# A two-block transformer kernel on one core: thirty-odd elementwise passes of the second block change from GpSimd to VectorE

## The chip, the cores and the metric

The kernel runs on 1 core of one Trainium2 chip. The metric is the device time of one execution in microseconds (us). The core has TensorE (PE in the profile, its weight loads PEld), VectorE (DVE), ScalarE (ACT), GpSimd (POOL) and SyncE (SP, which only issues DMAs here); ACT issues some DMAs too.

## The reference, cut to what matters

The reference is two blocks on 256 tokens of width 1024, all in float32. The first block has two layers, each a mixer and a product-key expert layer (PEER) with layer norms between them. The second block, whose mixer this change is about, is one layer:

```python
h = rmsnorm(x, g_mix[i])
u = h @ w_in[i]                      # rwkv columns, mla columns, gates
y_rw = rwkv7_time_mix(u_rw, ...)     # a recurrence over 256 steps, both directions
y_mla = mla_mix(u_mla, ...)          # 8 heads of attention
merged = gates[:, :, 0] * (y_rw @ w_br_rwkv[i]) + gates[:, :, 1] * (y_mla @ w_br_mla[i])
x = x + merged @ w_out[i]
x = x + peer_ffn(rmsnorm(x, g_ffn[i]), ...)
x = x + (p[i] @ w_ple_proj[i]) * jax.nn.sigmoid(rmsnorm(x, g_ple[i]) @ w_ple_gate[i])
```

In `rwkv7_time_mix` the projection `u` is first mixed with its two neighbours in time, `u + mu * (0.5 * (prev + next) - u)`, and the recurrence per head and direction is

```python
state = state * w_t + sa * b_t + v_t * k_t      # sa = state @ a_t
out_t = state @ r_t
```

with `a = -kk`, `b = kk * a`, decays `w`, and `kk` a normalized `k`.

## The kernel before, in words

**Split weights.** Every large product runs as three float32r matmuls: a weight tile `raw` is split into a high half `whi` (a cast on ACT, L111) and a low half `wlo = raw - whi` (a subtraction, L113), and TensorE adds whi·xhi, whi·xlo and wlo·xhi. `split(raw, lo)` at L106 takes a letter: "v" puts the subtraction on VectorE, anything else on GpSimd. `tm_halves` and `tm` (L183 and L191) pass a string of such letters that is gone through in turn. `raw` has 2 buffers of 2048 columns, `whi` and `wlo` 4 buffers each of 1024 columns.

**The end of the first block.** `layernorm` (L290) with `then` set goes over the two token halves tb = 0, 1: residual and statistics on VectorE (L299 to L302), four passes of scale and shift (L312, L313), then an rms norm whose transposed halves become `x` (`rmsnorm_tb`, `transposed_tb`). After tb = 0 it calls `ple_proj` (L277), which multiplies the per-layer embedding by two weight splits, and splits the four weight pieces of the mla projection ahead of their use (L318).

**The second block's projections.** `block2` loads eight pieces of `rw_fm` and splits each into two (the last into one): `weights(i)` at L660 names the engine. `shifted(i, dst)` at L666 runs the matmuls of piece i into a bank of PSUM, splits piece i + 1 ahead, copies the bank to `up` on ACT (L674) and does the neighbour mix on VectorE (L675 to L680). `cut` calls it for k, r and v, and between these calls the start of the first `prep` and the normalization `unit` are issued.

**The recurrence.** It is done in four rounds (two directions by two token halves). `prep(d, tb)` at L802 makes a round's operands: decays (`lw`, a scan `b`, exponentials `e3`), `AR` (L841 and L842), `bt` (L845, L846), `kt` (L856 to L858) and a running `ksum` (L860). `batch` at L885 inverts a triangular system per half of the heads by four doublings, each a mask on GpSimd (L922, L925), matmuls on TensorE (L928, L933), an addition on VectorE (L934) and a transpose (L938). `rwkv` at L1041 interleaves the two `batch` generators of a round with the `prep` of the next round; every third step it also advances the attention (`mla`, L1083).

**The order.** Each engine runs its own instructions strictly in the order in which they stand in its queue; the framework sets that order from the dependencies as it records the program, so that moving an operation to another engine also shifts its neighbours. A wait at the head of a queue holds all behind it.

Of the kernel before, what the change touches and what calls it, by code (L numbers as in the profile page):

```python
# [42 lines left out]
class Kern:  # L43
# [233 lines left out]
    def ple_proj(self, half, W):  # L277

        self.pd = self.dram.tile([4, 128, 512], F32, name="pd", tag="pd")
        pT = [t.rearrange("p (c t) -> p c t", c=2) for t in self.p_halves]  # L280
        for d in range(2):
            p = [self.bank("a") for _ in range(2)]
            self.tm(p, W["ple_proj"][d:d + 1], pT, "p")
            for tb in range(2):
                t = half("proj")
                self.nc.scalar.copy(t, p[tb])
                self.nc.sync.dma_start(self.pd[tb * 2 + d], t)

    def layernorm(self, half, h, acc, W, layer, k, then=None):

        nc = self.nc
# [3 lines left out]
        for tb in range(2):  # L295
            z = h[tb]
            st = self.strm.tile([128, 2, 6], F32, name="lnst", tag="lnst", bufs=2)
            for d in range(2):
                nc.vector.scalar_tensor_tensor(z[d], z[d], ALPHA, acc[tb][d], op0=ALU.mult, op1=ALU.add)  # L299
                nc.vector.bn_stats(st[:, d], z[d])  # L300
            mv = self.strm.tile([128, 3], F32, name="lnmv", tag="lnmv", bufs=2)
            nc.vector.bn_aggr(mv[:, 0:2], st.rearrange("p a b -> p (a b)"))  # L302
            self.rstd(mv[:, 1:2], 1e-5)
            if then is None:
                nc.vector.scalar_tensor_tensor(mv[:, 2:3], mv[:, 0:1], -1.0, mv[:, 1:2], op0=ALU.mult, op1=ALU.mult)
                self.scaled(z, z, mv[:, 1:2], mv[:, 2:3])
                n = 2 * layer + k
                self.transposed_tb(half, z, x, tb, self.lnc[:, n, 0], self.lnc[:, n, 1])
                self.store_h(tb, h, (layer, k))
            else:  # L310
                for d in range(2):
                    nc.vector.scalar_tensor_tensor(z[d], z[d], mv[:, 0:1], grow[d], op0=ALU.subtract, op1=ALU.mult)  # L312
                    nc.vector.scalar_tensor_tensor(z[d], z[d], mv[:, 1:2], brow[d], op0=ALU.mult, op1=ALU.add)  # L313
                self.rmsnorm_tb(half, h, x, tb, then)
                self.store_h(tb, h)
                if tb == 0:
                    self.ple_proj(half, W)
                    self.mla_halves = list(self.tm_halves(W["mla_tm"], "p", 416))  # L318
        return x

    def rms_scale(self, half, h, tb):
# [295 lines left out]
    def block2(self, x, W):  # L617
        nc = self.nc
        sub, add, mul = ALU.subtract, ALU.add, ALU.mult
        mm = nc.tensor.matmul  # L620
        with ExitStack() as st:
# [37 lines left out]

            def weights(i):  # L660
                raw = self.load(W["rw_fm"][i]) if i < 7 else self.load(W["rw_last"], 1024)
                return [self.split(raw[:, k * 1024:k * 1024 + 1024], "pv"[k] if i else "vp"[k]) for k in range(2 if i < 7 else 1)]

            ahead = [weights(0)]

# [136 lines left out]
            def prep(d, tb):  # L802
# [36 lines left out]
                yield  # L839
                AR = mx.tile([128, 4, 2, 128], F32, name="AR", tag="AR", bufs=2)  # L840
                nc.vector.scalar_tensor_tensor(AR[:, :, 0], lw, -1.0, kkT[tb], op0=mul, op1=mul)  # L841
                nc.gpsimd.tensor_tensor(AR[:, :, 1], b, rT[tb], op=mul)  # L842
                yield
                bt, kt = g4("bt"), g4("kt")
                nc.gpsimd.tensor_tensor(flat(bt), flat(kkT[tb]), flat(a), op=mul)  # L845
                nc.gpsimd.tensor_tensor(flat(bt), flat(bt), flat(e3), op=mul)  # L846
                yield
                for f in range(4):
                    nc.vector.tensor_scalar(a[:, f], a[:, f], 1.0, k_a[:, f:f + 1], op0=sub, op1=mul)
# [7 lines left out]
                yield  # L857
                nc.vector.tensor_tensor(flat(kt), flat(kd), flat(e3), op=mul)  # L858
                if not fresh:
                    nc.gpsimd.tensor_tensor(flat(ksum[tb]), flat(ksum[tb]), flat(kd), op=add)  # L860
                yield
                AY = [gran("AY").rearrange("p (f a c) -> p f a c", f=2, a=4) for _ in range(2)]
                Bt, Kt = [gran("Bt") for _ in range(2)], [gran("Kt") for _ in range(2)]
# [836 lines left out]
```

## Time and profile before

| what | value |
| --- | --- |
| median of 3 runs | 3317.68 us (3301.85, 3317.68, 3320.57) |
| the profiled execution, its own time | 3306.54 us |
| its span, first to last instruction | 3304.8 us |
| mean granted clock of TensorE | 0.977 of full speed |
| busy: PE, PEld, DVE, ACT, POOL | 95%, 86%, 76%, 49%, 28% of the span |

The profile names a group by line, engine, operation and tiles (out<-in), with its count, busy time, mean, and the idle time of the engine just before it with what ended that idle time ("<-"). A timeline row is: start in us from the span's start, duration in us, engine, line, operation, tiles, shape, count of instructions merged into the row, and in brackets an idle time before it. The duration of a row runs from when the engine took the instruction to its end, so that time in which an engine sits on an instruction that cannot proceed is in it.

The second block's mixer lies between 1960 us and about 2345 us of the span. Everything before it is the first block, and what follows is the gates, the output projection, the second block's PEER layer and the tail.

### The profile page before, as it was taken

How to read it: one execution, taken by the hardware profiler on the slowest of the kernel's cores; microseconds unless marked ns; L12 is line 12 of the kernel's file. 1: busy time of each engine (PE TensorE's matmuls, PEld its weight loads, DVE VectorE, ACT ScalarE, POOL GpSimd, SP SyncE). 2: the span in 40 equal slices, each digit the busy share in tenths (PEclk: the TensorE clock that was granted, in tenths of full speed). 3: DMA queues.
4: the chain of work that ended last, by engine and by line, in shares of the span. 5: the costliest groups of instructions: out<-in, count | busy, mean ns of one | idle time of the engine just before them, and what ended most of it. 6: DMA issues, size and time to landing. Idle time of an engine off the chain costs nothing.

```text
span 3304.8 us, 56194 instructions
## 1 busy us (share of the span) xinstructions
PE 3151.0 (95%) x22652; PEld 2827.8 (86%) x22652; DVE 2510.2 (76%) x4203; ACT 1631.2 (49%) x2450; POOL 916.4 (28%) x424
## 2 busy tenths in 40 slices
PE   8999999999999999999999997889999999999998
PEld 7899888887888799988887877778789998888887
DVE  6687989897456696888898556654569698999855
ACT  5554444444455554544444445554455444444445
POOL 1610132234213540023324223242143003323230
PEclk9999999999999999999999998999999999999999
DMA  5455555555653456565556653000455555655664
GB/s 214 166 202 203 193 195 205 198 203 201 226 199 129 153 181 214 189 208 193 195 195 220 220 181 141 1 1 14 166 179 184 211 193 195 207 199 199 231 210 156
DMA packets 119525, 592.24 MB, mean 179 GB/s; under 512 B 14304, under 2 KB 14688, under 8 KB 59104
## 3 DMA queue, kind: packets, MB, share of 16 engines
q1 hardware_dynamic: 96768, 549.18, 48.1%
q10 hardware_dynamic: 22496, 39.47, 3.2%
q8 instruction: 177, 2.90, 0.3%
q14 instruction: 84, 0.69, 0.1%
HBM read 548.23 MB, written 40.37 MB: 178 GB/s over the span
## 4 chain that ended last, share of the span: by engine, by line
PE 68%; DVE 17%; DMA 6%; POOL 3%; ACT 3%; issue 3%; ACTq 0%; DVEq 0%; SPq 0%; POOLq 0%
PE ps_b L119 10%; PE ps_a L1537 10%; PE ps_b L121 10%; PE ps_b L120 10%; PE ps_a L1539 10%; PE ps_a L1538 9%; DVE wlo L113 3%; DVE A L1435 2%; DMA raw<-u 2%; DVE clo L1466 2%; PE ps_c L1448 2%; POOL wlo L113 2%; DMA back<-away 1%; DVE Z L1443 1%; ACT whi L111 1%
## 5 line engine op out<-in xcount | busy, mean ns | idle before, releaser
L111 ACT CAST whi<-raw 128x1024 fp32r<-128x1024 f32 x941 | 976.6, 1048 | 1244.3 <-DMA raw<-v 318.2
L113 POOL TENSOR_TENSOR wlo<-raw,whi 128x1024 fp32r<-128x1024 f32 (+1 forms) x294 | 767.0, 2623 | 1945.6 <-ACT whi L111 1358.4
L121 PE MATMUL ps_b<-xThi,wlo 128*128 128x256 f32 x3608 | 1029.9, 285 | 29.1 <-POOL wlo L113 16.1
L119 PE MATMUL ps_b<-xThi,whi 128*128 128x256 f32 x3608 | 1034.6, 287 | 10.4 <-ACT whi L111 8.8
L120 PE MATMUL ps_b<-xTlo,whi 128*128 128x256 f32 x3608 | 1027.8, 285 | 0.3 <-DVE xTlo L144 0.3
L113 DVE TENSOR_TENSOR wlo<-raw,whi 128x1024 fp32r<-128x1024 f32 x647 | 804.2, 1247 | 223.3 <-ACT whi L111 219.9
L121 PEld LDWEIGHTS ps_b<-xThi,wlo 128*128 128x128 f32 x3608 | 699.0, 194 | 31.9 <-POOL wlo L113 17.7
L119 PEld LDWEIGHTS ps_b<-xThi,whi 128*128 128x128 f32 x3608 | 699.5, 194 | 15.5 <-ACT whi L111 9.0
L120 PEld LDWEIGHTS ps_b<-xTlo,whi 128*128 128x128 f32 x3608 | 699.0, 194 | 4.6 <-DVE xTlo L144 0.6
L1537 PE MATMUL ps_a<-whi,chi 128*128 128x512 f32 x1536 | 620.0, 404 | 0.3 <-ACT chi L1464 0.3
L1539 PE MATMUL ps_a<-whi,clo 128*128 128x512 f32 x1536 | 609.8, 397 | 6.0 <-DVE clo L1466 6.0
L1538 PE MATMUL ps_a<-wlo,chi 128*128 128x512 f32 x1536 | 608.4, 396 | 0.2 <-DVE wlo L113 0.2
L1539 PEld LDWEIGHTS ps_a<-whi,clo 128*128 128x128 f32 x1536 | 290.3, 189 | 75.5 <-DVE clo L1466 7.3
L1435 DVE TENSOR_TENSOR A<-iota,comb 128x2048 f16<-128x2048 f16 x192 | 330.1, 1719 | 21.4 <-PE ps_c L1448 21.2
L1538 PEld LDWEIGHTS ps_a<-wlo,chi 128*128 128x128 f32 x1536 | 290.9, 189 | 62.6 <-DVE wlo L113 0.5
L1537 PEld LDWEIGHTS ps_a<-whi,chi 128*128 128x128 f32 x1536 | 291.1, 190 | 61.7 <-ACT chi L1464 0.5
L1466 DVE TENSOR_TENSOR clo<-back,chi 128x512 fp32r<-128x512 f32 x126 | 159.5, 1266 | 88.4 <-ACT chi L1464 86.0
L1443 DVE TENSOR_TENSOR Z<-B,comb 128x512 f16<-128x512 f16 x384 | 204.7, 570 | 0.0
L1462 DVE TENSOR_TENSOR back<-back,G 128x512 f32<-128x512 f32 x126 | 100.2, 798 | 89.2 <-DMA back<-away 89.2
L1453 DVE SCALAR_TENSOR_TENSOR G<-ps_c,G 128x256 f32<-128x256 f32 x384 | 150.0, 414 | 21.2 <-ACT G L1452 20.2
L1537 PE MATMUL ps_a<-whi,xThi 128*128 128x512 f32 (+1 forms) x320 | 132.0, 413 | 14.6 <-ACT xThi L180 14.1
L1452 ACT ACTIVATE G<-ps_c 128x256 f32<-128x256 f32 x384 | 134.0, 378 | 11.2 <-PE ps_a L1539 0.4
(517 smaller groups left out, 3359.1 us busy)
## 6 DMA issues: line engine op xcount, KB each, us to landing
raw<-u SPq DMA_DIRECT2D x192, 1024.0 KB, 4.9
raw<-v SPq DMA_DIRECT2D x192, 1024.0 KB, 4.8
away<-gone ACTq DMA_DIRECT2D x126, 256.0 KB, 2.3
back<-away SPq DMA_DIRECT2D x126, 256.0 KB, 2.7
raw<-wq SPq DMA_DIRECT2D x24, 1024.0 KB, 4.8
raw<-c_tm SPq DMA_DIRECT2D x8, 1024.0 KB, 4.8
raw<-c_fm SPq DMA_DIRECT2D x8, 1024.0 KB, 4.8
raw<-gates_tm SPq DMA_DIRECT2D x8, 1024.0 KB, 4.8
```

The source lines that it names most:

```text
L111: self.nc.scalar.copy(hi, raw)
L113: eng.tensor_tensor(low, raw, hi.bitcast(F32), op=ALU.subtract)
L119: mm(out, whi, xhi, start=start, stop=False, skip_group_check=True)
L120: mm(out, whi, xlo, start=False, stop=False, skip_group_check=True)
L121: mm(out, wlo, xhi, start=False, stop=stop, skip_group_check=True)
L1435: nc.vector.tensor_tensor(A, self.iota2.unsqueeze(1).to_broadcast([128, 16, 64, 2]), cv[:, 0].to_broadcast([128, 16, 64, 2]), op=eq)
L1443: nc.vector.tensor_tensor(Z[:, :, i], B, cv[:, 2 + i].to_broadcast([128, 16, 16, 2]), op=mul)
L1453: nc.vector.scalar_tensor_tensor(Gt, pv[:, 1], 2.0 ** -15, Gt, op0=mul, op1=add)
L1466: nc.vector.tensor_tensor(clo, C, chi.bitcast(F32), op=sub)
L1537: mm(out, xhi, whi, start=start, stop=False, skip_group_check=True)
L1538: mm(out, xhi, wlo, start=False, stop=False, skip_group_check=True)
L1539: mm(out, xlo, whi, start=False, stop=stop, skip_group_check=True)
```

## The change

Four edits, in the second block's mixer and the end of the first block's last layer norm:

- `ple_proj` (L283) and the mla pieces (L318) split with "v" in place of "p": two subtractions of 128x1024 and four of 128x832 change from GpSimd to VectorE.
- `weights` (L662) calls `split` without a letter, which means VectorE: eight subtractions of 128x1024 change over, seven stay on VectorE as before.
- In `prep`, the products of L842, L845 and L846 change over, in each of four rounds.
- The addition to `ksum` (L860) changes over, in the two rounds that have it.

GpSimd keeps the masks (L922, L925), the memsets, the state's addition (L1024) and the products of `finish` (L1062, L1065).

```diff
@@ ple_proj
-            self.tm(p, W["ple_proj"][d:d + 1], pT, "p")
+            self.tm(p, W["ple_proj"][d:d + 1], pT)
@@ layernorm
-                    self.mla_halves = list(self.tm_halves(W["mla_tm"], "p", 416))
+                    self.mla_halves = list(self.tm_halves(W["mla_tm"], "v", 416))
@@ block2, weights
-                return [self.split(raw[:, k * 1024:k * 1024 + 1024], "pv"[k] if i else "vp"[k]) for k in range(2 if i < 7 else 1)]
+                return [self.split(raw[:, k * 1024:k * 1024 + 1024]) for k in range(2 if i < 7 else 1)]
@@ block2, prep
-                nc.gpsimd.tensor_tensor(AR[:, :, 1], b, rT[tb], op=mul)
+                nc.vector.tensor_tensor(AR[:, :, 1], b, rT[tb], op=mul)
-                nc.gpsimd.tensor_tensor(flat(bt), flat(kkT[tb]), flat(a), op=mul)
-                nc.gpsimd.tensor_tensor(flat(bt), flat(bt), flat(e3), op=mul)
+                nc.vector.tensor_tensor(flat(bt), flat(kkT[tb]), flat(a), op=mul)
+                nc.vector.tensor_tensor(flat(bt), flat(bt), flat(e3), op=mul)
-                    nc.gpsimd.tensor_tensor(flat(ksum[tb]), flat(ksum[tb]), flat(kd), op=add)
+                    nc.vector.tensor_tensor(flat(ksum[tb]), flat(ksum[tb]), flat(kd), op=add)
```

On GpSimd, from the start of the second block to the first masks of the recurrence, this is the difference of its queue (- before, + changed, no sign both):

```order
-L113 TENSOR_TENSOR wlo<-raw,whi 128x1024 x4
 L726 CAST pair_21615<-k_rw 128x256
-L113 TENSOR_TENSOR wlo<-raw,whi 128x1024 x4
-L842 TENSOR_TENSOR AR<-b,rT 128x4x128
-L845 TENSOR_TENSOR bt<-kkT,a 128x512
-L846 TENSOR_TENSOR bt<-bt,e_21923 128x512
 L925 TENSOR_TENSOR gm<-L,k_rw 128x4x128
 L922 TENSOR_TENSOR E_22278<-gm,k_rw 128x512
 L922 TENSOR_TENSOR E_22287<-gm,k_rw 128x512
```

All eight subtractions and the first round's three products have left GpSimd's queue there; one cast and then the masks remain.

On VectorE, in the projections of k and r (a later piece of `shifted`, with its neighbour mix L675 to L680):

```order
 L676 COPY sh<-up 128x2x2
+L113 TENSOR_TENSOR wlo<-raw,whi 128x1024
 L677 SCALAR_TENSOR_TENSOR sh<-sh,up 128x512
 L113 TENSOR_TENSOR wlo<-raw,whi 128x1024
 L680 SCALAR_TENSOR_TENSOR two<-sh,rw_mu,up 128x256 x2
+L113 TENSOR_TENSOR wlo<-raw,whi 128x1024
 L819 TENSOR_SCALAR lw<-lw 128x512
 L675 TENSOR_TENSOR sh<-up 128x2x254
 L676 COPY sh<-up 128x2x2
 L677 SCALAR_TENSOR_TENSOR sh<-sh,up 128x512
+L113 TENSOR_TENSOR wlo<-raw,whi 128x1024
```

The subtractions of the following pieces now stand between the steps of the neighbour mix, two of them inside it.

On VectorE, in the second round of the recurrence, from the first addition to N on (L849 makes the factor for `kt`, L934 is the addition that the next transposes wait for):

```order
 L934 TENSOR_TENSOR N<-N,ps_b 128x512
 L841 SCALAR_TENSOR_TENSOR AR<-lw,kkT 128x4x128
-L849 TENSOR_SCALAR a<-a,rw_cols 128x128 x3
+L845 TENSOR_TENSOR bt<-kkT,a 128x512
 L934 TENSOR_TENSOR N<-N,ps_b 128x512
-L849 TENSOR_SCALAR a<-a,rw_cols 128x128
+L846 TENSOR_TENSOR bt<-bt,e_22838 128x512
+L842 TENSOR_TENSOR AR<-b,rT 128x4x128
+L849 TENSOR_SCALAR a<-a,rw_cols 128x128 x4
```

Between the two additions to N there is now one product where three passes of L849 were; L849 has gone behind the second addition.

## Rows read from the trace of the kernel before

**Rows 1.** Two stretches: length, busy PE, PEld, DVE, ACT, POOL, clock, DMA.

```profile
1959.90:1992.60 32.70, 23.63 (x96) 18.20 (x95) 26.54 (x38) 17.09 (x36) 13.75 (x7) 0.90 0.53 186
1992.60:2050.40 57.80, 44.96 (x333) 43.95 (x332) 43.65 (x57) 32.84 (x65) 27.10 (x21) 0.91 0.39 132
```

**Rows 2.** What TensorE waited for, 1960 to 2335 us: us, times, longest.

```profile
PE ps_c L928 <- POOL gm L925: 11.4, 5, 4.1
PE ps_c L938 <- DVE N L934: 10.4, 3, 4.1
PE ps_c L758 <- ACT q L778: 6.7, 1, 6.7
```

**Rows 3.** Timeline of GpSimd, late in the projections.

```profile
2043.34 5.32 POOL L113 TENSOR_TENSOR wlo<-raw,whi 128x1024 fp32r<-128x1024 f32 x2 [9.13 <-ACT whi L111]
```

**Rows 4.** Timeline of VectorE: three passes beside no GpSimd work, one beside rows 3.

```profile
2004.98 1.22 DVE L113 TENSOR_TENSOR wlo<-raw,whi 128x1024 fp32r<-128x1024 f32 x1
...
2034.99 0.69 DVE L677 SCALAR_TENSOR_TENSOR sh<-sh,up 128x512 f32<-128x512 f32 x1
...
2036.74 0.87 DVE L680 SCALAR_TENSOR_TENSOR two<-sh,rw_mu,up 128x256 f32<-128x256 f32 x2
...
2044.00 4.93 DVE L680 SCALAR_TENSOR_TENSOR two<-sh,rw_mu,up 128x256 f32<-128x256 f32 x2
```

**Rows 5.** Groups of GpSimd, 1960 to 2112 us: the subtractions.

```profile
L113 POOL TENSOR_TENSOR wlo<-raw,whi 128x1024 fp32r<-128x1024 f32 x10 | 26.7, 2684 | 60.5 <-ACT whi L111 54.1 <-PE ps_b L121 6.5
...
L113 POOL TENSOR_TENSOR wlo<-raw,whi 128x832 fp32r<-128x832 f32 x4 | 8.3, 2102 | 8.9 <-ACT whi L111 8.9
```

**Rows 6.** Groups of GpSimd, 1990 to 2330 us: the products of `prep`.

```profile
L845 POOL TENSOR_TENSOR bt<-kkT,a 128x512 f32<-128x512 f32 x4 | 6.0, 1495 | 3.6 <-DVE kkT L784 3.6
...
L846 POOL TENSOR_TENSOR bt<-bt,e 128x512 f32<-128x512 f32 x4 | 5.4, 1348 | 0.3
L842 POOL TENSOR_TENSOR AR<-b,rT 128x512 f32<-128x512 f32 x4 | 5.1, 1272 | 14.8 <-ACT b L838 14.8
...
L860 POOL TENSOR_TENSOR ksum<-ksum,a 128x512 f32<-128x512 f32 x2 | 3.0, 1521 | 3.2 <-DVE st L1126 2.2 <-DVE a L856 1.1
```

**Rows 7.** Groups of VectorE, 1960 to 2112 us.

```profile
L680 DVE SCALAR_TENSOR_TENSOR two<-sh,rw_mu,up 128x256 f32<-128x256 f32 x12 | 11.3, 984 | 0.1
L113 DVE TENSOR_TENSOR wlo<-raw,whi 128x1024 fp32r<-128x1024 f32 x7 | 10.7, 1527 | 0.9 <-ACT whi L111 0.9
L313 DVE SCALAR_TENSOR_TENSOR page<-page,lnmv 128x512 f32<-128x512 f32 x4 | 8.4, 2142 | 0.0
L677 DVE SCALAR_TENSOR_TENSOR sh<-sh,up 128x512 f32<-128x512 f32 x7 | 7.0, 997 | 0.2
L312 DVE SCALAR_TENSOR_TENSOR page<-page,lnmv 128x512 f32<-128x512 f32 x4 | 6.7, 1693 | 0.1
L675 DVE TENSOR_TENSOR sh<-up 128x508 f32<-128x508 f32 x7 | 6.6, 946 | 4.7 <-ACT up L674 4.4
...
L680 DVE SCALAR_TENSOR_TENSOR lwa<-sh,rw_mu,up 128x256 f32<-128x256 f32 x2 | 2.9, 1490 | 0.0
...
L226 DVE RECIPROCAL lnmv<-lnmv 128x1 f32<-128x1 f32 x2 | 0.3, 160 | 2.9 <-ACT lnmv L225 2.9
```

**Rows 8.** Issues of the mla weights: count, KB each, us to landing.

```profile
raw<-mla_tm SPq DMA_DIRECT2D x2, 832.0 KB, 4.8
```

**Rows 9.** Timeline of VectorE, second round of the recurrence.

```profile
2163.21 3.72 DVE L849 TENSOR_SCALAR a<-a,rw_cols 128x128 f32<-128x128 f32 x3 [1.16 <-POOL bt L845]
2166.85 0.67 DVE L934 TENSOR_TENSOR N<-N,ps_b 128x512 f32<-128x512 f32 x1
```

**Rows 10.** Timeline of GpSimd and of TensorE in the same round.

```profile
2160.34 1.16 POOL L925 TENSOR_TENSOR gm<-L,k_rw 128x512 f32<-128x512 f32 x1 [1.11 <-PE ps_b L933]
...
2168.49 3.62 PE L928 MATMUL ps_c<-N,gm 128*128 128x128 f32 x16
...
2182.94 2.02 PE L928 MATMUL ps_c<-N,gm 128*128 128x128 f32 x16
```

## The prediction

> **What bounds the kernel now.** I read the busy time of stretches first, then what TensorE waits for, then the timelines of VectorE and GpSimd side by side, and last the groups, for the prices. The edits touch only 1960 to about 2260 us of the span; the first block before and the second block's PEER layer behind keep their instructions and their order.
>
> In the two stretches that hold the end of the last layer norm and the projections, TensorE is busy for 23.63 of 32.70 us and for 44.96 of 57.80 us, VectorE for 26.54 and 43.65 [rows 1]. So TensorE is not full there, and VectorE looks nearly so. What the reader is to see is that VectorE's busy time there is not work. One subtraction of 128x1024 takes it 1.22 us, one pass of L677 over 128x512 takes 0.69, a pair of L680 takes 0.87 [rows 4]. At 2044.00 the same pair of L680 takes 4.93 us; GpSimd began two subtractions at 2043.34 that run 5.32 us, to 2048.66, and the pair ends at 2048.93, 0.27 us later [rows 3, 4]. VectorE sat on the pair until GpSimd was done. Such stretched passes are everywhere that GpSimd subtracts: L680 has a mean of 984 ns where 435 is its own (half of 0.87), L677 one of 997, L312 of 1693, L313 of 2142 [rows 7].
>
> This reaches TensorE as a wait: 6.7 us in one piece for the squares of `unit` (L778), which stand behind the stretched pair at 2044; and 10.4 us in three waits for the addition L934 in the recurrence, one per round that has a `prep` beside it [rows 2]. In the second round, three passes of L849 take 3.72 us behind GpSimd's `bt`, and L934 stands after them in the queue [rows 9]. Another 11.4 us go to the masks themselves (L925) [rows 2]; those stay on GpSimd and I expect that wait to stay.
>
> **The change in prices.** Off GpSimd go ten subtractions of 128x1024, 26.7 us, and four of 128x832, 8.3 us [rows 5], and fourteen products of 128x512, 6.0 + 5.4 + 5.1 + 3.0 = 19.5 us [rows 6]: 54.5 us of GpSimd, part of it time in which GpSimd in turn sat on VectorE. Onto VectorE come 10 x 1.22 = 12.2 us; 4 x 0.99 = 4.0 us, an estimate by columns from 1.22 x 832/1024; and 14 x 0.69 = 9.7 us, with L677's row as the nearest, a pass of the same size with two SBUF operands [rows 4]. Sum 25.9 us. What comes back to VectorE is the stretch of its other passes. I go by stages.
>
> **The layer norm's end** (1959.9 to 1992.6). L312 and L313, eight passes, took 6.7 + 8.4 = 15.1 us [rows 7]; alone they would take 8 x 0.69 = 5.5. Relief 9.6. Added: two subtractions of 1.22 and four of 0.99, 6.4 us. If all of the added lies on the path the gain is 3.2, if none, 9.6. The new queue puts the two between L313 of the first token half and the second half's passes, and the four ahead of the reciprocal L226. There VectorE already waited 2.9 us, because ScalarE's casts for the same four pieces stand ahead of the square root [rows 7]; those casts remain, and following the queue with single prices about 1.1 us of the added work falls into that time. Gain 9.6 - 6.4 + 1.1 = **4.3 us**. SP's queue changes here too: both mla loads now stand behind the two stores of h, and each needs a raw buffer that VectorE's subtraction frees. I cost that at nothing, since the casts that use them stand behind the transposes of the first token half; without that cover it is up to one landing, 4.8 us [rows 8].
>
> **The projections** (1992.6 to 2050.4). Relief, group by group: the fourteen L680 took 11.3 + 2.9 = 14.2 against 14 x 0.435 = 6.1, so 8.1; L677 7.0 against 7 x 0.69, 2.2; L675 6.6 against the same 4.8, 1.8; the seven subtractions that were VectorE's already 10.7 against 8.5, 2.2 [rows 4, 7]. Together 14.3. Added: 8 x 1.22 = 9.8. The gain is 4.5 if all of it lies on the path and 14.3 if none does. VectorE idles for 14.15 of the 57.80 us [rows 1], and the path runs through ScalarE's copies (`up`, L674) as often as through VectorE. Following the queue piece by piece, the first subtraction of the first piece no longer sits behind GpSimd's, one and another of the new ones stand inside the neighbour mix and delay it, some fall into waits for `up`; about 3.5 us of the added are so absorbed. Gain 14.3 - 9.8 + 3.5 = **8.0 us**, nearer the low end because nearly every new subtraction stands ahead of a step of the mix.
>
> **`unit` and the first `prep`** (2050 to 2071). With the pair at 2044 whole again, TensorE no longer sits idle for the 6.7 us before L758 [rows 2]. That wait is already in the 8.0; what comes on top is that the 20-odd matmuls between the two `unit` steps then run at the upper clock. Bounds: nothing, and the 6.7 us once more; I take 2.3, by following ScalarE's steps with TensorE's share at full speed. AR and `bt` are three products one after the other at 0.69 in place of 1.27, 1.50 and 1.35 [rows 6], but `bt` now stands behind L841 on VectorE: 0.9. Together **3.2 us**.
>
> **The recurrence.** In each of three rounds L934 gets back most of its wait. In the second, the new queue has one product between the two additions, 0.69 us, where three passes of L849 and GpSimd's `bt` were. Behind the first addition a mask may get in first, 1.16 us [rows 10]. So the wait falls from 10.4/3 = 3.5 us to about 0.8: 3 x 2.7 = **8.0 us**. Queued behind the products are L849, L856 and L858, and behind these the last copies of `kz` on ScalarE; the next addition waits for a whole further doubling on TensorE (transpose, two products), which covers them; without that cover they cost what they take on VectorE, two passes of 0.69 and L849. Bounds: nothing, if masks and products take turns as L849 did; 10.4, and on top of it the clock: sixteen L928 took 3.62 us right behind such a wait and 2.02 in full flow [rows 10], 1.6 us a round, 4.8 us. I leave the clock out of the sum and in the range.
>
> **A rule against it.** The Trainium skill, "Perfetto Trace Analysis", section "Optimizing Scalar/DVE Operations", says that where the vector engine is saturated, some work may be moved off it, to ScalarE or even to GpSimd; this change goes the other way in the one place where VectorE looks saturated. By that the 25.9 us would be a loss (the second rival has its time). The same section adds that the two share a read port, so that moving work between them might not help. By the first half the sum is +25.9, by rows 3 and 4 it is a gain.
>
> **Sum.** 4.3 + 8.0 + 3.2 + 8.0 = 23.5 us, 0.7%. The low bounds give 3.2 + 4.5 + 0 + 0 = 7.7; the upper ones, clock included, cannot all hold at once, and I take 31 as the end. The profiled execution took 3306.54 us (its span and 1.74 us around it), so by it 3283.0. It lies 11.1 us below the median of the runs, 3317.68; the four executions shown (3301.85, 3306.54, 3317.68, 3320.57) have a mean of 3311.7. I set the forecast against that mean: 3311.7 - 23.5 = **3288 us**.
>
> **Rivals.** (1) *The relief lies beside the path.* TensorE has about 45 us of work in the 57.8 us of the projections, ScalarE's copies pace the mix, and freed masks of GpSimd run into the chain's VectorE passes, 1.16 us each, twice a round. Then only the layer norm's low end and the low end of the projections are left: 7.7 us, 3304 from the same mean, within 0.5% of no change. For it: VectorE's idle 14 us there [rows 1]. Against: the 6.7 us and 10.4 us of TensorE [rows 2], which hang on stretched passes directly. (2) *VectorE's queue becomes the bound.* All 25.9 us stand in order ahead of the passes that others wait for, and the stretch given back was time in which the queue would have waited for ScalarE anyway: 3311.7 + 25.9 = 3338 us. It decides from the point where the relief on the path falls below 25.9; the groups above show 9.6 + 14.3 of relief in the first two stages against 16.2 added, so a third of that relief has to be empty for these stages to break even, and all of it for the full price. That the change does not do what it says can be left out: the queues printed above have moved.
>
> **Chances.** 0.5%, 16.6 us, is about what a measurement of this kernel can tell from no change. Forecast, a gain of 17 us or more: 0.68. Rival 1, and what is between it and the forecast: 0.27. Rival 2 and other losses: 0.05. The range takes the gain from 10 to 31 us and the spread of the executions: from 3301.9 - 31 = 3271 to 3317.7 - 10 = 3308.
>
> **What would show it.** Right: L680 at 0.44 us, L677 at 0.69, L312 and L313 at about 0.7 in their groups; no wait of TensorE before L758; L934's wait at a few us in place of 10.4; L925's wait near 11; the recurrence's first `gm` some 15 us earlier in the span. Wrong: passes of VectorE still stretched though GpSimd is idle, an `up` copy that no longer leads the mix but waits for it, or TensorE's waits moved to L121 or L1538 for a low half by VectorE.

## The result, and the profile after

The changed kernel takes 3272.43 us (median of six executions, 3268.48 to 3284.21); the kernel before, with as many, 3306.75 us (3301.85 to 3320.57). The ratio is 0.9892, 95% interval 0.9866 to 0.9919: 1.1% faster. The forecast was 3288 us with a range of 3271 to 3308; the direction was right and the time lies at the range's low end.

The first block's part of the span differs by up to 13 us between profiled executions of kernels that are alike in it (the layer norm's first L299 starts between 1955.2 and 1968.1 us in all the traces here). So I compare lengths of stages, each from one instruction's start to another's: the layer norm's end from the first L299 to L642 (the first step of the projections' angles), the projections with `unit` and the first `prep` from there to the first `gm` (L901), the recurrence from there to the first L1055. The first bound is loose: VectorE stands idle ahead of L642 for 4.2 to 6.4 us in the traces here, by the profile mostly until a DMA of small columns (`rw_cols`, `rw_mu`) has landed. The end of the last `xTlo` (L181) ahead of it, which the prediction took as the end of this stage, is tight, and I use it where the stage's own gain counts. Busy time by windows, first the kernel before, then the changed one; the columns are the window, its length, busy us and instructions of PE, PEld, DVE, ACT and POOL, granted clock, DMA share and GB/s:

```profile
1959.89:1996.96 37.07, 28.00 (x111) 22.43 (x110) 26.55 (x38) 19.12 (x39) 18.07 (x13) 0.86 0.50 174
1996.96:2075.73 78.77, 60.67 (x433) 58.40 (x432) 58.59 (x86) 44.57 (x88) 26.93 (x17) 0.89 0.31 111
2075.73:2320.77 245.04, 221.52 (x1908) 201.67 (x1906) 136.13 (x210) 127.24 (x265) 79.77 (x66) 0.94 0.02 5
```

```profile
1961.84:1994.17 32.33, 27.23 (x117) 22.46 (x115) 23.09 (x45) 19.18 (x39) 4.72 (x12) 0.89 0.59 197
1994.17:2060.03 65.86, 56.96 (x425) 54.76 (x426) 49.65 (x97) 43.54 (x86) 0.67 (x1) 0.92 0.36 132
2060.03:2291.00 230.97, 215.77 (x1908) 194.44 (x1906) 135.21 (x223) 127.66 (x267) 65.53 (x55) 0.98 0.02 6
```

The three stages give 37.07 - 32.33 = 4.7, 78.77 - 65.86 = 12.9 and 245.04 - 230.97 = 14.1 us, together 31.7; the spans of the two traces differ by 31.1. What the reader is to see: with 28 passes added (the title's thirty-odd are 28) VectorE runs more instructions in every stage and is busy for less time (26.55 to 23.09, 58.59 to 49.65, 136.13 to 135.21), and in the recurrence TensorE, with the same 1908 matmuls, is busy 5.8 us less at a mean granted clock of 0.98 in place of 0.94 and idle 15.2 in place of 23.5 us.

VectorE's groups of the changed kernel from 1960 to 2090 us (busy us, mean ns of one | idle before), beside [rows 7]:

```profile
L680 DVE SCALAR_TENSOR_TENSOR two<-sh,rw_mu,up 128x256 f32<-128x256 f32 x12 | 5.3, 475 | 0.0
L677 DVE SCALAR_TENSOR_TENSOR sh<-sh,up 128x512 f32<-128x512 f32 (+1 forms) x8 | 5.2, 655 | 0.2
L312 DVE SCALAR_TENSOR_TENSOR page<-page,lnmv 128x512 f32<-128x512 f32 x4 | 2.9, 745 | 0.1
L313 DVE SCALAR_TENSOR_TENSOR page<-page,lnmv 128x512 f32<-128x512 f32 x4 | 2.8, 746 | 0.0
```

L680 fell from 984 to 475 ns, L312 and L313 from 1693 and 2142 to about 745. The pair of L680 that took 4.93 us [rows 4], in VectorE's timeline of the changed kernel:

```profile
2035.06 0.87 DVE L680 SCALAR_TENSOR_TENSOR two<-sh,rw_mu,up 128x256 f32<-128x256 f32 x2
```

TensorE's waits of the changed kernel from 1955 to 2305 us (total, times, longest):

```profile
PE ps_c L928 <- POOL gm L925: 11.4, 5, 4.1
PE ps_b L119 <- ACT up L674: 3.6, 1, 3.6
...
PE ps_b L121 <- DVE wlo L113: 1.9, 1, 1.9
...
PE ps_c L938 <- DVE N L934: 1.4, 3, 0.7
...
PE ps_a L1538 <- DVE wlo L113: 1.2, 1, 1.2
PE ps_c L758 <- ACT q L778: 1.0, 1, 1.0
```

Further waits of TensorE in the kernel before, from 1960 to 2335 us, beside [rows 2]:

```profile
PE ps_b L166 <- ACT page L264: 3.8, 1, 3.8
PE ps_b L121 <- DVE wlo L113: 2.8, 1, 2.8
...
PE ps_a L1538 <- POOL wlo L113: 1.7, 2, 1.6
...
PE ps_b L119 <- ACT up L674: 1.6, 1, 1.6
```

L934's wait fell from 10.4 to 1.4 us, `unit`'s from 6.7 to 1.0, and the 3.8 us of L166, which in the layer norm stands behind the stretched passes, are gone. The masks' wait stayed at 11.4. The wait for the copy `up` rose from 1.6 to 3.6 us. Low halves were waited for in both kernels: 2.8 and 1.7 us before, 1.9 and 1.2 now, and now VectorE makes them all.

### The profile page after: what moved, and what is told of

It reads as the page before. It is cut to its first block, busy times and chain, and to the rows that moved or that the text cites. A ratio compares the mean times of both kernels' runs of the same rounds, so it can differ in the third digit from the quotient of the medians.

```text
span 3273.7 us, 56183 instructions
## 1 busy us (share of the span) xinstructions
PE 3141.6 (96%) x22652; PEld 2818.2 (86%) x22652; DVE 2482.2 (76%) x4231; ACT 1632.3 (50%) x2450; POOL 866.6 (26%) x396
## 4 chain that ended last, share of the span: by engine, by line
PE 70%; DVE 16%; DMA 5%; issue 3%; ACT 3%; POOL 2%; ACTq 0%; SPq 0%; DVEq 0%; POOLq 0%
PE ps_b L119 10%; PE ps_b L121 10%; PE ps_b L120 10%; PE ps_a L1537 10%; PE ps_a L1539 10%; PE ps_a L1538 10%; DVE wlo L113 4%; DMA raw<-u 2%; DVE A L1435 2%; DVE clo L1466 2%; PE ps_c L1448 2%; DMA back<-away 1%; POOL wlo L113 1%; ACT whi L111 1%; DVE Z L1443 1%
## 5 line engine op out<-in xcount | busy, mean ns | idle before, releaser
L113 POOL TENSOR_TENSOR wlo<-raw,whi 128x1024 fp32r<-128x1024 f32 x280 | 735.9, 2642 | 1876.0 <-ACT whi L111 1301.6
L121 PE MATMUL ps_b<-xThi,wlo 128*128 128x256 f32 x3608 | 1030.5, 286 | 26.8 <-POOL wlo L113 14.9
L113 DVE TENSOR_TENSOR wlo<-raw,whi 128x1024 fp32r<-128x1024 f32 (+1 forms) x661 | 815.8, 1238 | 228.7 <-ACT whi L111 223.1
L119 PEld LDWEIGHTS ps_b<-xThi,whi 128*128 128x128 f32 x3608 | 700.5, 194 | 15.7 <-ACT whi L111 7.2
L1538 PE MATMUL ps_a<-wlo,chi 128*128 128x512 f32 x1536 | 609.2, 397 | 0.1
L1538 PEld LDWEIGHTS ps_a<-wlo,chi 128*128 128x128 f32 x1536 | 291.7, 190 | 62.9 <-DVE wlo L113 0.6
L1435 DVE TENSOR_TENSOR A<-iota,comb 128x2048 f16<-128x2048 f16 x192 | 318.4, 1658 | 25.3 <-PE ps_c L1448 25.0
L1443 DVE TENSOR_TENSOR Z<-B,comb 128x512 f16<-128x512 f16 x384 | 217.7, 605 | 0.0
L1466 DVE TENSOR_TENSOR clo<-back,chi 128x512 fp32r<-128x512 f32 x126 | 144.1, 1143 | 92.1 <-ACT chi L1464 91.9
L1537 PE MATMUL ps_a<-whi,xThi 128*128 128x512 f32 (+1 forms) x320 | 131.4, 411 | 15.8 <-ACT xThi L180 14.1
L1448 PE MATMUL ps_c<-Z,A 128*128 128x64 f16 x3072 | 125.9, 194 | 15.0 <-DVE G L1453 15.0
```

Source lines behind the costliest of these rows:

```text
L113: eng.tensor_tensor(low, raw, hi.bitcast(F32), op=ALU.subtract)
L119: mm(out, whi, xhi, start=start, stop=False, skip_group_check=True)
L121: mm(out, wlo, xhi, start=False, stop=stop, skip_group_check=True)
L1435: nc.vector.tensor_tensor(A, self.iota2.unsqueeze(1).to_broadcast([128, 16, 64, 2]), cv[:, 0].to_broadcast([128, 16, 64, 2]), op=eq)
L1443: nc.vector.tensor_tensor(Z[:, :, i], B, cv[:, 2 + i].to_broadcast([128, 16, 16, 2]), op=mul)
L1448: nc.tensor.matmul(pg[:, k * 64:k * 64 + 64], A[:, t].rearrange("p b f -> p (b f)"), Z[:, t].rearrange("p i b f -> p (i b f)"), start=True ...
```

## The experiments

Two theories. **Exclusion:** a VectorE pass with SBUF operands cannot run beside a GpSimd subtraction or product; the gain is the other passes' own time given back, and what hung on them. **Late results:** what counted was only that GpSimd delivered the moved results late. All lengths are from one profiled execution each; times and ratios against the kernel before are from several.

| kernel | layer norm's end | projections | recurrence | TensorE idle in it | median us | ratio |
| --- | --- | --- | --- | --- | --- | --- |
| before | 37.1 | 78.8 | 245.0 | 23.5 | 3306.75 | |
| changed | 32.3 | 65.9 | 231.0 | 15.2 | 3272.43 | 0.9892 |
| e1 layer norm's part | 31.0 | 77.7 | 244.7 | 23.5 | 3301.99 | 0.9984 |
| e2 projections' part | 37.6 | 65.0 | 242.0 | 22.5 | 3290.08 | 0.9953 |
| e3 `prep`'s part | 37.9 | 78.1 | 231.0 | 15.2 | 3291.16 | 0.9958 |
| e8 only `bt` | 37.7 | 78.9 | 231.4 | 15.9 | 3294.69 | 0.9953 |
| e4 changed + 8 on GpSimd | 32.3 | 76.1 | 230.9 | 15.1 | 3287.74 | 0.9947 |
| e9 the same, one operand | 32.5 | 69.0 | 230.9 | 15.2 | 3279.46 | 0.9903 |
| e10 the same by VectorE | 31.8 | 73.1 | 231.0 | 15.2 | 3278.50 | 0.9923 |
| e5 mask later | 32.4 | 63.6 | 224.7 | 12.0 | 3268.14 | 0.9864 |
| e6 first mask by VectorE | 31.3 | 64.5 | 218.8 | 7.3 | 3262.13 | 0.9860 |
| e7 all masks by VectorE | 32.1 | 64.7 | 215.7 | 4.9 | 3261.25 | 0.9853 |
| e11 the rest by VectorE too | 33.2 | 65.5 | 216.2 | 5.5 | 3259.49 | 0.9853 |
| e12 changed, again | 32.2 | 66.5 | 230.9 | 15.1 | 3272.71 | 0.9899 |

Six of these (the changed kernel, e5, e6, e7, e11, e12) have the same instructions in the first two stages; their sum there is 95.8 to 98.7 us. So a difference below about 3 us in these two columns tells nothing. Two lengths are tighter: to the last `xTlo` the layer norm's end takes 32.6 to 33.4 us in the kernels whose GpSimd makes its low halves (before, e2, e3, e8) and 26.7 to 27.5 in all others, and the recurrence of the changed kernel, e3, e4, e9, e10 and e12 takes 230.9 to 231.0.

### The three parts alone (e1, e2, e3)

e1 has the first two edits of the diff, e2 that of `weights`, e3 the four in `prep`; short, against the kernel before:

```diff
-            self.tm(p, W["ple_proj"][d:d + 1], pT, "p")
+            self.tm(p, W["ple_proj"][d:d + 1], pT)
...
-                    self.mla_halves = list(self.tm_halves(W["mla_tm"], "p", 416))
+                    self.mla_halves = list(self.tm_halves(W["mla_tm"], "v", 416))
```

> The kernel before with one part of the change alone: the low halves of the ple projection's and of mla_tm's weights by VectorE. T1 (a GpSimd operation and a VectorE pass that reads two operands from SBUF exclude each other, so the gain is the other passes' own time given back): L312 and L313 fall from 1693 and 2142 ns to about 0.75 us each as in the changed kernel, the last xTlo of the layer norm comes about 4 to 6 us earlier relative to the layer norm's start, and all of it reaches the end: a gain of 4 to 6 us, while the stretches behind keep their lengths (L934's waits near 10 us). R1 (what counts is only that GpSimd's results come earlier): no wait for a low half of GpSimd stands in the trace of before here, so the gain is under 2 us.

```diff
-                return [self.split(raw[:, k * 1024:k * 1024 + 1024], "pv"[k] if i else "vp"[k]) for k in range(2 if i < 7 else 1)]
+                return [self.split(raw[:, k * 1024:k * 1024 + 1024]) for k in range(2 if i < 7 else 1)]
```

> The kernel before with one part of the change alone: the low halves of the second block's projections' weights by VectorE. T1: L680 at about 0.45 us, L677 and L675 near 0.69, the wait before L758 falls from 6.7 to about 1 us, the projections get 9 to 11 us shorter, and the recurrence behind keeps its length: a gain of 9 to 13 us in all. R1: TensorE waits for no low half of GpSimd in the projections of before, so under 3 us.

```diff
-                nc.gpsimd.tensor_tensor(AR[:, :, 1], b, rT[tb], op=mul)
+                nc.vector.tensor_tensor(AR[:, :, 1], b, rT[tb], op=mul)
...
-                nc.gpsimd.tensor_tensor(flat(bt), flat(kkT[tb]), flat(a), op=mul)
-                nc.gpsimd.tensor_tensor(flat(bt), flat(bt), flat(e3), op=mul)
+                nc.vector.tensor_tensor(flat(bt), flat(kkT[tb]), flat(a), op=mul)
+                nc.vector.tensor_tensor(flat(bt), flat(bt), flat(e3), op=mul)
...
-                    nc.gpsimd.tensor_tensor(flat(ksum[tb]), flat(ksum[tb]), flat(kd), op=add)
+                    nc.vector.tensor_tensor(flat(ksum[tb]), flat(ksum[tb]), flat(kd), op=add)
```

> The kernel before with one part of the change alone: the preparation products (AR, bt, ksum) by VectorE. T1: L849's passes are no longer stretched, L934's wait falls from 10.4 to 1 to 3 us and, since TensorE then stops for less, the sixteen L928 that ran 3.62 us run about 2.0: a gain of 12 to 16 us, of which about 9 are the wait and the rest the clock. By the prediction's own term, with the clock left out, 8 to 9 us. The three parts alone should add up to the whole change, 31 to 34 us, if they do not share anything; under 25 would mean that one part is only worth something with the others.

Measured: ratios of 0.9984 (0.9972 to 0.9996), 0.9953 (0.9937 to 0.9968) and 0.9958 (0.9940 to 0.9975), which are 0.16, 0.47 and 0.42% of about 3308 us: 5.3, 15.5 and 13.9 us. Together 34.7; the whole change, at 0.9892, is 35.7. The parts add up within their intervals, and each gains where its own edit lies: e1 6.1 us in the layer norm's end, e2 13.8 in the projections, e3 14.0 in the recurrence. In e1 L312 and L313 fell as in the whole change, here in VectorE's groups from 1955 to 2000 us:

```profile
L312 DVE SCALAR_TENSOR_TENSOR page<-page,lnmv 128x512 f32<-128x512 f32 x4 | 2.9, 746 | 0.1
L313 DVE SCALAR_TENSOR_TENSOR page<-page,lnmv 128x512 f32<-128x512 f32 x4 | 2.8, 748 | 0.0
```

To the last `xTlo` the stage takes 26.8 us, as in the changed kernel, in place of 32.6. The rival in e1's expectation (R1) rested on a wrong reading: TensorE did wait in this stage for GpSimd's low halves, the 1.7 us of L1538 shown above, and in e1 it waits 1.2 us there for VectorE's. Late results could so explain 1.7 of the 5.8 us at most. e2 gave somewhat more than 9 to 13 us. One point of its expectation was missed: the recurrence behind it did get shorter, by 3.0 us, as L934's wait fell from 10.4 to 8.8 us without an edit there. VectorE's and GpSimd's queues stand in the same order there, and the granted clock was 0.96 in place of 0.94; why, no run here shows. e3's waits from 1955 to 2310 us and its recurrence by window:

```profile
PE ps_c L938 <- DVE N L934: 1.4, 3, 0.7
```

```profile
2072.60:2303.60 231.00, 215.77 (x1908) 194.43 (x1906) 135.07 (x222) 126.42 (x265) 65.49 (x55) 0.98 0.02 6
```

It has the changed kernel's recurrence to a few hundredths: of 14.0 us, 8.3 are idle time (23.5 to 15.2) and 5.8 busy time of the same matmuls (221.5 to 215.8) at a higher granted clock.

### Which of the four lines (e8)

```diff
-                nc.gpsimd.tensor_tensor(flat(bt), flat(kkT[tb]), flat(a), op=mul)
-                nc.gpsimd.tensor_tensor(flat(bt), flat(bt), flat(e3), op=mul)
+                nc.vector.tensor_tensor(flat(bt), flat(kkT[tb]), flat(a), op=mul)
+                nc.vector.tensor_tensor(flat(bt), flat(bt), flat(e3), op=mul)
```

> The kernel before with the two products of bt alone (L845, L846) by VectorE; AR's product and ksum stay on GpSimd. If L934's wait comes from the passes of L849 that VectorE holds behind GpSimd's bt, these two lines carry nearly all of what the four products' lines gave together (recurrence 245.1 us before, 231.0 with all four): L934's wait falls from 10.4 us to 1 to 4 us and the recurrence to 232 to 236 us. Rival: AR's product and ksum on GpSimd hold up other passes in their place, and the recurrence stays above 238 us.

Recurrence 231.4 us, a little below the 232 to 236 expected: the two lines of `bt` carry 13.6 of the 14.0 us, though AR's product and `ksum` stayed on GpSimd. e8's waits from 1955 to 2310 us and its recurrence:

```profile
PE ps_c L938 <- DVE N L934: 2.9, 2, 1.7
```

```profile
2083.90:2315.30 231.40, 215.54 (x1909) 195.32 (x1907) 134.86 (x217) 127.04 (x265) 73.67 (x60) 0.98 0.02 6
```

So the recurrence's term was one chain, the one the prediction had named: `bt` on GpSimd, L849 held behind it, L934 behind L849 [rows 9]. Held in two ways, as VectorE's groups of the recurrence show, before and in the changed kernel:

```profile
L849 DVE TENSOR_SCALAR a<-a,rw_cols 128x128 f32<-128x128 f32 x12 | 11.0, 963 | 4.2 <-POOL bt L845 4.2
```

```profile
L849 DVE TENSOR_SCALAR a<-a,rw_cols 128x128 f32<-128x128 f32 x12 | 2.6, 277 | 0.0
```

L849 overwrites `a`, which GpSimd's L845 reads, so VectorE first stood idle for 4.2 us until L845 was done: that is GpSimd being late, as the second theory has it. Then the passes took 11.0 us in place of 2.6 beside GpSimd's next operations: that is the stretch. e3 and e8 took both away at once, and how the 14 us divide between them is not shown.

### Useless work put back beside the projections (e4, e9, e10)

e4, against the changed kernel; e9 has instead of the subtraction `nc.gpsimd.tensor_scalar(..., hi, 0.0, None, op0=mul)`, e10 the same subtraction with `nc.vector`. Line numbers behind 660 are two to five higher in these kernels (L680 is L685, L677 is L682):

```diff
+            bz = mx.tile([128, 4, 2, 128], F32, name="bz")
...
-                return [self.split(raw[:, k * 1024:k * 1024 + 1024]) for k in range(2 if i < 7 else 1)]
+                out = [self.split(raw[:, k * 1024:k * 1024 + 1024]) for k in range(2 if i < 7 else 1)]
+                hi = out[0][0].bitcast(F32)
+                nc.gpsimd.tensor_tensor(bz.rearrange("p f q t -> p (f q t)"), hi, hi, op=sub)
+                return out
...
-            bz, kz = (mx.tile([128, 4, 2, 128], F32, name=n) for n in ("bz", "kz"))
+            kz = mx.tile([128, 4, 2, 128], F32, name="kz")
```

> The changed kernel with eight subtractions of 128x1024 added on GpSimd in the projections, each of a piece's high half from itself (zeros into bz, which is set to zero later anyway), so that the output is unchanged; nothing on the path waits for them soon. T1: VectorE's passes that fall beside them are stretched again (L680, L677, L675 and L113 by up to about 2.5 us each), and the projections lose 8 to 16 us: 3281 to 3289 us from 3272. R1: GpSimd is idle there and nobody waits for these results, so within 3 us of the changed kernel.

> The same as the kernel with eight added subtractions on GpSimd, but each is a multiplication of the high half by 0.0: one operand read in place of two, the same size, still nobody waits for it soon. If any long GpSimd operation that reads SBUF holds up VectorE's passes with two SBUF operands, L680 is stretched here as well (over 1 us a pass beside one) and the projections lose 5 to 12 us against the changed kernel. If it takes two operands on both engines, L680 stays at 0.48 us and the time is within 3 us of the changed kernel.

> The changed kernel with the same eight useless subtractions as before, this time by VectorE itself: eight more passes of 1.22 us, 9.8 us of VectorE's time in the projections. On GpSimd they took the changed kernel's projections from 98.2 to 108.4 us (the layer norm's end to the first gm). By the prediction's way of counting a part of them falls into idle time and the rest, about 6 us, lies on the path: 102 to 107 us. If the same work costs less on the busy VectorE than on the idle GpSimd, that is the reason for the change's gain in one pair of numbers. Rival: VectorE's queue is the bound, all 9.8 us count and more waits come on top, 108 us or more.

The first two stages together take 108.4 us in e4, 101.5 in e9 and 104.9 in e10, against 95.8 to 98.7 without the additions. Eight operations whose results nobody waits for cost about 11 us (9.7 to 12.6) on the idle GpSimd and about 7.5 (6.2 to 9.1) on the busy VectorE. That the first is a cost is clear, in the times too: e4's ratio of 0.9926 to 0.9968 does not meet the changed kernel's 0.9866 to 0.9919. That it is more than on VectorE is likely and not shown: the two single traces lie 3.5 us apart, about as far as kernels alike there do, and e10's ratio of 0.9898 to 0.9949 overlaps e4's. Nor is it a buffer of `whi` that the additions hold: in e4's trace no engine waits for L666. GpSimd's and VectorE's timelines of e4:

```profile
2027.62 1.90 POOL L666 TENSOR_TENSOR bz<-whi 128x1024 f32<-128x1024 f32 x1 [3.83 <-ACT whi L111]
```

```profile
2027.69 2.51 DVE L685 SCALAR_TENSOR_TENSOR two<-sh,rw_mu,up 128x256 f32<-128x256 f32 x2
```

GpSimd begins 0.07 us before the pair and ends at 2029.52; the pair ends at 2030.20, 0.68 us later, and has taken 2.51 us for its 0.87. No data passes between the two. So in the projections exclusion holds, and late results are not needed. It is not only passes with two operands that are held. The first two of the eight additions, GpSimd's and VectorE's timelines of e4:

```profile
1987.53 3.86 POOL L666 TENSOR_TENSOR bz<-whi 128x1024 f32<-128x1024 f32 x2 [0.43 <-ACT whi L111]
```

```profile
1988.49 1.08 DVE L642 CAST cs<-posi 128x256 f32<-128x256 int32 x1 [5.53 <-DMA rw_cols<-rw_cols]
1989.61 1.93 DVE L643 TENSOR_SCALAR cs<-cs,k_rope 128x256 f32<-128x256 f32 x1
```

Each reads one tensor in SBUF, L643 a column of factors besides, and in the changed kernel they take 0.29 and 0.35 us. In e9, with one operand read by GpSimd:

```profile
2033.96 3.40 POOL L666 TENSOR_SCALAR bz<-whi 128x1024 f32<-128x1024 f32 x1 [4.12 <-ACT whi L111]
```

```profile
2033.48 1.22 DVE L113 TENSOR_TENSOR wlo<-raw,whi 128x1024 fp32r<-128x1024 f32 x1
2034.62 1.66 DVE L685 SCALAR_TENSOR_TENSOR two<-sh,rw_mu,up 128x256 f32<-128x256 f32 x2
```

The pair takes 1.66 us and ends at 2036.28, 1.08 us before GpSimd does: its first pass takes 1.26 us, its second 0.47, its own time, though GpSimd's row goes on. So VectorE is held for a part of GpSimd's time and not shut out for all of it. e9 fell between its two expectations: over its ten L685 the mean is 644 ns, against 475 in the changed kernel and 1227 in e4. In e10 nothing is stretched, and the eight passes take their own time (VectorE's groups from 1984 to 2056 us):

```profile
L666 DVE TENSOR_TENSOR bz<-whi 128x1024 f32<-128x1024 f32 x8 | 9.7, 1212 | 0.0
L685 DVE SCALAR_TENSOR_TENSOR two<-sh,rw_mu,up 128x256 f32<-128x256 f32 x10 | 4.4, 476 | 0.1
```

### The masks that stayed (e5, e6, e7, e11)

11.4 us of TensorE's time still wait for L925. Against the changed kernel, e5 moves E5's mask, e6 the first of each round's masks, e7 all, and e11 on top of e7 the state's sums and the bonus products (L1024, L1062, L1065, each `nc.gpsimd` to `nc.vector`):

```diff
e5
-                nc.gpsimd.tensor_tensor(u4(E5), gm[:, :, 0], bc(5, 1 - d), op=mul)
...
                     nc.scalar.copy(Ps, u4(pP))
                     yield
+                    if k == 1:
+                        nc.gpsimd.tensor_tensor(u4(E5), gm[:, :, 0], bc(5, 1 - d), op=mul)
e6
-                    nc.gpsimd.tensor_tensor(E, u4(L), bc(k, d), op=mul)
+                    (nc.vector if k == 1 else nc.gpsimd).tensor_tensor(E, u4(L), bc(k, d), op=mul)
e7
-                nc.gpsimd.tensor_tensor(u4(E5), gm[:, :, 0], bc(5, 1 - d), op=mul)
+                nc.vector.tensor_tensor(u4(E5), gm[:, :, 0], bc(5, 1 - d), op=mul)
...
-                    nc.gpsimd.tensor_tensor(E, u4(L), bc(k, d), op=mul)
+                    nc.vector.tensor_tensor(E, u4(L), bc(k, d), op=mul)
```

> The changed kernel with the mask E5 (L922), which is read only at the end of a round, issued behind the first doubling instead of ahead of the first masks. If the 11.4 us that TensorE still waits for L925 come from GpSimd's queue (two L922 of 2.73 us stand ahead of the second half's first mask), the wait falls to 2 to 5 us and the kernel gets 6 to 9 us faster than the changed one, 3263 to 3266 us. Rival: the second masks then stand behind L922 and the wait only moves to them: within 2 us of the changed kernel.

> The changed kernel with the first of a round's masks (L925 at k = 1, eight in all) by VectorE; the other masks stay on GpSimd. Eight more passes of 0.69 us for VectorE. The wait for L925 by GpSimd goes (11.4 us) and 1 to 3 us for VectorE's own mask come in: 7 to 10 us faster than the changed kernel, 3262 to 3265 us. By the exclusion alone, with GpSimd's L922 now beside VectorE's passes of that moment, up to 3 us of it are given back.

> The changed kernel carried to its end: all masks of the recurrence (forty passes, 27.6 us at 0.69) by VectorE as well, GpSimd with nothing but the state's sums there. Exclusion as the whole story: no pass is stretched any more, the wait for L925 goes and the kernel gets 8 to 12 us faster than the changed one, 3260 to 3264 us. The prediction's second rival (VectorE's queue becomes the bound), here in the place where TensorE is bound: the additions L934 stand behind the masks again, their wait comes back to 5 to 10 us, and the time is within 3 us of the changed kernel or above it.

> The kernel with all masks by VectorE, and with what was left to GpSimd from the recurrence's start to its end by VectorE too: the state's sums (L1024) and bonus products (L1062, L1065). The sums are a step between two steps of VectorE: 0.72 us and two handovers become two passes of about 0.42. Expected 1 to 4 us faster than with the masks alone (recurrence 215.7 us to 212 to 215). Rival: the sums' cross-engine steps were hidden by TensorE's other matmuls, within 1 us. Either way 45 us or more below the kernel before, and at least 10 us below the changed kernel beside it.

> The changed kernel itself, on the same chip as the kernel with no masks left on GpSimd, so that the two can be compared: 0.987 to 0.992 of the kernel before, as in its first comparison.

e5's wait fell only to 8.0 us, where 2 to 5 were expected, and the recurrence by 6.3; e6's to 4.0 and by 12.2. In e7 it is all but gone. The waits from 1955 to 2310 us, of e5, e6 and e7:

```profile
PE ps_c L927 <- POOL gm L924: 8.0, 5, 4.1
```

```profile
PE ps_c L928 <- DVE gm L925: 4.0, 5, 1.2
```

```profile
PE ps_c L938 <- DVE N L934: 2.5, 5, 0.9
...
PE ps_c L928 <- DVE gm L925: 0.5, 1, 0.5
```

e7's recurrence by window:

```profile
2059.10:2274.80 215.70, 210.77 (x1908) 190.42 (x1907) 142.54 (x263) 126.83 (x267) 10.46 (x14) 1.00 0.02 6
```

Forty more passes on VectorE (263 instructions, 223 in the changed kernel) add 7.3 us to its busy time, not the 27.6 that they were expected to take, and the stage gets 15.3 us shorter, with a granted clock of 1.00. e11 is no further on in the recurrence (216.2): its sums were hidden, as the rival had it. Beside the repeated changed kernel (e12: 3272.71 us, ratio 0.9884 to 0.9914) e11 stands at 3259.49 us (0.9835 to 0.9870), 13.2 us lower; the intervals do not meet. e7, 3261.25 us and 0.9837 to 0.9870, is as good with fewer edits: **both, at 0.9853 against 0.9899, beat the repeated changed kernel by about 0.4% and the kernel before by 1.5%.**

## Why the prediction was right, and where terms were too small

**What bounds the kernel.** Right. Much of VectorE's busy time was stretch: 28 passes were added to it, and in the three stages its busy time fell from 221.3 to 208.0 us (207.8 in e12). The whole program's sum can't tell this: it was 2510.2 us before, 2482.2 in the changed kernel and 2504.5 in the same kernel again, e12. Each sign listed as "right" came, or nearly: L680 475 ns, L312 and L313 745, `unit`'s wait 1.0 us where none was forecast, L934's 1.4, L925's 11.4, the first `gm` 15.7 us earlier in the span. Of the signs listed as "wrong", TensorE does wait for low halves by VectorE, 1.9 and 1.2 us, but it waited 2.8 and 1.7 for low halves before.

The first three terms by the prediction's own bounds, which are the end of the last `xTlo` and the start of `unit`'s first L758, before and after:

```profile
1959.89:1992.48 32.59, 23.52 (x96) 18.08 (x95) 26.55 (x38) 17.09 (x36) 13.74 (x6) 0.90 0.53 187
1992.48:2050.44 57.96, 45.08 (x335) 44.07 (x333) 43.69 (x58) 32.84 (x65) 27.11 (x21) 0.91 0.39 132
2050.44:2075.73 25.29, 20.08 (x114) 18.68 (x115) 14.91 (x30) 13.76 (x25) 4.15 (x3) 0.79 0.14 57
```

```profile
1961.84:1988.61 26.77, 21.68 (x95) 17.26 (x94) 23.09 (x44) 17.08 (x36) 0.00 (x0) 0.92 0.65 222
1988.61:2037.43 48.82, 45.33 (x352) 44.38 (x351) 35.67 (x65) 32.70 (x65) 5.39 (x13) 0.97 0.46 161
2037.43:2060.03 22.60, 17.18 (x97) 15.58 (x98) 13.98 (x33) 12.94 (x23) 0.00 (x0) 0.77 0.14 57
```

**Layer norm's end, 4.3 us.** Measured 5.8, and e1, to 26.8 us, shows the same; the term was somewhat small. It let 1.1 us of the added work fall into VectorE's 2.9 us of idle time before L226 [rows 7], and in the changed kernel none of that idle time is left.

**Projections, 8.0 us.** Measured 9.1, the term nearly held. Its way of counting what the added passes cost is not contradicted: the prediction let 9.8 - 3.5 = 6.3 us of eight added subtractions lie on the path, and eight more of them in e10 cost 6.2 to 9.1.

**`unit` and the first `prep`, 3.2 us.** Measured 2.7; the size nearly held, its reason did not. TensorE is idle for 5.2 us of the stage before and 5.4 after, at a granted clock of 0.79 and 0.77. What is shorter is its busy time, 20.08 and 17.18 us, with 17 matmuls fewer (114 and 97), and the projections ahead hold 17 more (335 and 352): they now run ahead of L758, where TensorE had stood idle for 6.7 us. The upper clock, to which I had put down 2.3 us, hardly came. The stretch of the matmuls between the two L758, before and after:

```profile
2052.17:2056.58 4.41, 4.41 (x21) 4.41 (x22) 1.48 (x4) 3.68 (x6) 0.00 (x0) 0.50 0.45 184
```

```profile
2038.35:2042.22 3.87, 3.87 (x23) 3.87 (x22) 2.29 (x6) 3.64 (x6) 0.00 (x0) 0.58 0.56 231
```

It is 0.5 us shorter, at a granted clock of 0.58 in place of 0.50, and 0.50 is the lower of its two levels.

**The recurrence, 8.0 us: the term that was too small.** Measured 14.1. The wait's part was right in size: idle time fell by 8.3 us where 8.0 stood, and a mask did get in behind the first addition, as [rows 10] had suggested. In the changed kernel, GpSimd and VectorE in the second round:

```profile
2139.74 1.23 POOL L925 TENSOR_TENSOR gm<-L,k_rw 128x512 f32<-128x512 f32 x1 [0.34 <-PE ps_b L933]
```

```profile
2139.87 1.64 DVE L845 TENSOR_TENSOR bt<-kkT,a 128x512 f32<-128x512 f32 x1
2141.44 0.67 DVE L934 TENSOR_TENSOR N<-N,ps_b 128x512 f32<-128x512 f32 x1
```

L845 begins 0.13 us behind the mask and takes 1.64 us; L934 still comes only half a microsecond late for TensorE. The prediction had put the wait down to the stretched passes alone; VectorE's 4.2 us of standing idle for `bt`, shown with e8, came on top of them. What was left out of the sum, though the prediction had its row, is the clock: 1.6 us a round, 4.8 in all, kept for the range. It came in full: the same matmuls are busy for 5.8 us less. With it in the sum the forecast would have been 23.5 + 4.8 = 28.3 against the 31.7 of the two traces.

**The start.** The forecast stood against 3311.7 us, the mean of the executions then shown. With six the median before is 3306.75: 5.0 of the 15.6 us by which 3288 missed 3272.4 are that, the rest is the sum (34.3 by the medians, 23.5 forecast).

**The rivals.** "Beside the path" gave 7.7 us and fell: 34. "VectorE's queue becomes the bound" fell twice, in the change and in e7, which put 27.6 us more of passes on it and gained. Only e10 shows such a price, where passes were added and no stretch was taken away.

**The rule weighed.** The Trainium skill, "Perfetto Trace Analysis", section "Optimizing Scalar/DVE Operations", says that where VectorE is saturated it may make sense to move some work off it, to GpSimd too. By that this change would lose; here it gained, since much of the busy time was made by the work that had been moved off. The same section says that the two share a read port, so that moving work between them might not help. e4 agrees, where the pair took 2.51 us beside GpSimd for its 0.87. The Trainium skill, "SBUF — State Buffer", section "SBUF: two separate sides", says that of a GpSimd operation that reads SBUF and a VectorE pass with two SBUF inputs whichever starts first holds the shared ports for its whole instruction while the other blocks. e4's 2.51 us agrees; e9's 1.66 us, ended 1.08 us ahead of GpSimd, does not, and the measurement decides, as far as GpSimd's spans, which are rough, can show it.

## What to carry to other kernels

Before work goes from VectorE to GpSimd, or when it already has, look whether the passes beside it keep their own duration: VectorE's busy share cannot tell work from being held up, and a group whose mean is twice its shortest can. Work on an idle engine is not free; here eight operations that nobody waited for cost about 11 us, no less than the same work in the full queue. Where a wait of TensorE is removed, count the matmuls right behind it at the clock that the trace shows in full flow as well, not the wait alone.

## What the runs showed of the hardware that I had not expected

That with one GpSimd operand in place of two VectorE's passes are held far less (644 ns a pass of L685 in place of 1227, 475 undisturbed), though GpSimd's operation itself is longer (3.40 us in place of 1.90). That a VectorE pass that reads one tensor in SBUF is held beside GpSimd too: e4's L643 took 1.93 us in place of 0.35. And how far the granted clock goes along with the waits: 0.94 in the recurrence before, 0.98 with 8.3 us less idle, 1.00 with 18.6 us less, and the same 1908 matmuls took 221.5, 215.8 and 210.8 us.
